# Order of the sums in the recurrence's output batches of a hybrid MLA and RWKV-7 trunk

## The chip, the cores and the metric

The kernel runs on one core of one Trainium2 chip. The metric is the device time of one execution in microseconds, as the median of several runs.

## The reference, cut to what matters

Two layers work on 512 prompt frames and 64 frames of a running stream, with the same weights. A layer is a SwiGLU half-step, a token mixer, cross-attention into 256 memory tokens, and a second SwiGLU half-step. In the mixer eight MLA attention heads stand beside eight RWKV-7 heads. The part at issue is the RWKV-7 recurrence, per head with a 64 by 64 state:

```
def step(S, inp):
    r_t, w_t, k_t, v_t, kk_t, a_t = inp
    sa = einsum('bhvk,bhk->bhv', S, -kk_t)
    S = (S * w_t[:, :, None, :] + sa[..., None] * (kk_t * a_t)[:, :, None, :]
         + v_t[..., None] * k_t[:, :, None, :])
    return S, einsum('bhvk,bhk->bhv', S, r_t)
```

The output y of each token is the state after that token, read with r. The eight heads' outputs are then normalised, gated and projected together with the attention's.

## The kernel before, in words

All activations lie transposed, features on the partitions and the 576 frames along the free dimension. Nearly all large matmuls are done as three products of split operands (high by high, high by low, low by high; `mm3`, lines 314 to 316), and the weights are split as they arrive (lines 246 and 247).

The recurrence of `mixer` is done by chunks of 64 frames. There are nine of them in a layer: first the one of the running stream, which starts from a stored state, and then the eight of the prompt, of which the first has no state. `prepare(c)` makes what doesn't depend on the state: the masked products `A`, an inverse by three rounds (tiles `nd`, `R`, `RF`), the transposed keys `bkt` and the values, brought to the other half of the partitions (`VS`, `UV`). `advance(c, ...)` is the chain from state to state: `pz` (A with VS), copied to `Z`; `pu` (RF with Z), copied to `UV` in two halves, by ScalarE and by VectorE; `pS` (bkt with UV), which with the old state becomes the new one (`S`); and the outputs `py`, copied to `yt`. `py` has two terms where there is an old state: the state read with `ck` (64 rows are summed over), and `UV` read with `A` (128 rows). Then come the mean and the squares of the outputs (`pc`, `p8`).

Each of these products is a `batch`: eight heads, as four pairs `p4` with two heads `e` each. A head has 64 columns of one bank of PSUM, at `p4 * 64`, on the upper or the lower half of the partitions by `e`. So a batch is one bank with eight sums of 64 by 64 numbers. All are plain f32 matmuls; each leaves two records in the trace.

The banks of the chain and of the outputs come from one tag, `sm`, with two buffers; those of `prepare` from `pp` with one. While the chain runs, `more(n)` draws pieces of MLA attention and of the memory's keys and values into the same program order (tags `g`, `sc`, `tp`, `po`). The order of the instructions on each engine is not that of the program text: a planner lays it out at compile time by its own model of the times, with the program's order as priority, and each engine then works through its own queue in that order.

Of the kernel before, what the change touches and what calls it, by code (L numbers as in the profile page):

```python
# [131 lines left out]
def build(tc, I, O):  # L132
    nc = tc.nc
    PE, ACT, DVE, POOL, SP = nc.tensor, nc.scalar, nc.vector, nc.gpsimd, nc.sync
# [23 lines left out]
    def tile_(shape, tag, dt):  # L158
        pool, n = tags[tag]
        return pool.tile(shape, dt, tag=tag, name=tag, bufs=n)  # L160
# [7 lines left out]
    def ps1(tag="sm"):  # L168
        return tile_([128, 512], tag, F32)
# [6 lines left out]
    def half(e):  # L176
        return slice(64 * e, 64 * e + 64)
# [439 lines left out]
    def mixer(l, V, xn):  # L617
# [374 lines left out]

        def batch(tag, *terms):

            p = ps1(tag)
            for p4 in range(4):
                for e in range(2):
                    o = p[half(e), p4 * 64:p4 * 64 + 64]
                    for n, f in enumerate(terms):
                        PE.matmul(o, *f(p4, e), start=(n == 0), stop=(n == len(terms) - 1))  # L1000
            return p[:, 0:256].rearrange("p (h t) -> p h t", h=4)

        def quads(tag):
# [7 lines left out]
        def prepare(c):  # L1011
# [9 lines left out]
            for e in range(2):  # L1021
# [3 lines left out]
                DVE.tensor_tensor(out=A[:, e], in0=p, in1=C("mA").rearrange("p (e n) -> p e n", e=2)[:, e].unsqueeze(1).to_broadcast([128, 4, 128]), op=ALU.mult)  # L1025

            pn = batch("pp", lambda p4, e: (A[half(e), e, p4, aa], DD[half(e), p4]))
            nd = st([128, 4, 64], "nd")
            ACT.activation(out=nd, in_=pn, func=AF.Copy)
            R = DT  # L1030
            for j in range(3):
                p = batch("pp", lambda p4, e: (nd[half(e), p4], R[half(e), p4]))
                R = st([128, 4, 64], "RF" if j == 2 else "R")
                DVE.tensor_tensor(out=R, in0=p, in1=DT, op=ALU.add)
# [25 lines left out]
        def advance(c, ck, bkt, A, R, VS, UV, S, VSn):  # L1060
# [3 lines left out]
            if S is None:  # L1064
                pz = batch("sm", lambda p4, e: (A[half(1 - e), e, p4, aa], VS[half(1 - e), e, p4]))
            else:
                pz = batch("sm", lambda p4, e: (A[:, e, p4, aa], VS[:, e, p4]))
# [72 lines left out]
        for p4 in range(4):  # L1140
            t1 = st([128, T], "t1")
            for s in hs:
                p = ps1()[:, 0:HT]
# [6 lines left out]
            for s, tag in zip(hs, ("pp", "po")):  # L1150
                p = ps1(tag)[:, 0:HT]
# [346 lines left out]
```

## Time and profile before

| | |
|---|---|
| median of 3 runs | 2917.13 us (2910.97 to 2923.18) |
| profiled execution, its own time | 2916.22 us |
| its span | 2914.5 us |
| matmul, share of the span | 96% |
| VectorE, ScalarE, GpSimd | 73%, 47%, 13% |
| mean granted TensorE clock | 0.973 |

The profile is that of one execution. PE is TensorE's matmuls and PEld its weight loads, which overlap with them; DVE is VectorE, ACT is ScalarE, POOL is GpSimd. A busy share says that the engine had an instruction in work, not that it worked at full rate. The granted clock is told as a share of the full 2.4 GHz. Times in the trace are in us from the start of the span.

### The profile page before, as it was taken

To read this page: it belongs to the slowest core of one execution; us is meant where nothing else is said; L and a number is where in the kernel's file an instruction comes from. 1 tells how busy PE (TensorE), PEld (TensorE's weight loads), DVE (VectorE), ACT (ScalarE), POOL (GpSimd) and SP (SyncE) were. 2 spreads that over 40 slices of the span, in tenths; PEclk is the share of its full clock that TensorE was granted. 3 is DMA by queue.
4 is the path that set the end of the run, shared out by engine and by line. 5 is a ranking of instruction groups with operands and counts; after the bars stand their busy time and mean duration, and the time that the engine had idled before them with its cause. 6 is when DMAs were issued, how large, how long until landed. Compare 5 with 4: busy or idle time off the path is not lost.

```text
span 2914.5 us, 56004 instructions
## 1 busy us (share of the span) xinstructions
PE 2808.8 (96%) x22188; PEld 2681.1 (92%) x22188; DVE 2132.0 (73%) x4216; ACT 1370.1 (47%) x2813; POOL 380.6 (13%) x461
## 2 busy tenths in 40 slices
PE   6999999889999999999989999998999999899998
PEld 6999999878889889999989999997888899899998
DVE  8887776865657579777787777668555666787776
ACT  5544455344544545444444444653545445444444
POOL 4000013510000031000130000254000000400000
PEclk8999999989999999999989999998999999999999
DMA  4333333552233222222213222346332332222222
GB/s 168 109 124 105 102 124 110 139 143 81 86 102 123 70 80 87 95 95 88 81 58 102 87 87 91 131 107 159 110 90 88 110 120 66 79 88 87 89 94 69
DMA packets 187576, 293.22 MB, mean 101 GB/s; under 512 B 87066, under 2 KB 113050, under 8 KB 187138
## 3 DMA queue, kind: packets, MB, share of 16 engines
q1 hardware_dynamic: 185010, 285.46, 31.8%
q0 software_dynamic: 2304, 4.20, 0.5%
q8 instruction: 174, 2.85, 0.4%
q14 instruction: 88, 0.72, 0.1%
HBM read 250.36 MB, written 41.63 MB: 100 GB/s over the span
## 4 chain that ended last, share of the span: by engine, by line
PE 71%; DVE 4%; DMA 1%; ACT 1%; issue 1%; POOL 1%; SPq 0%; DVEq 0%; POOLq 0%; ACTq 0%
PE b L316 13%; PE b L314 13%; PE b L315 13%; PE sm L1000 4%; PE g L314 3%; PE g L316 3%; PE g L315 3%; PE mm L314 2%; PE mm L315 2%; PE mm L316 2%; PE pp L1000 2%; PE sc L314 1%; PE pp L1024 1%; PE sc L316 1%; PE sc L315 1%
## 5 line engine op out<-in xcount | busy, mean ns | idle before, releaser
L246 ACT ACTIVATE whi<-wraw 128x512 fp32r<-128x512 f32 (+1 forms) x520 | 321.4, 623 | 486.1 <-PE b L315 226.7
L316 PE MATMUL b<-s,wlo 128*128 128x288 f32 x1536 | 450.2, 295 | 0.0
L315 PE MATMUL b<-s,whi 128*128 128x288 f32 x1536 | 448.8, 293 | 0.0
L314 PE MATMUL b<-s,whi 128*128 128x288 f32 x1536 | 447.9, 295 | 0.0
L247 DVE TENSOR_TENSOR wlo<-wraw,whi 128x512 fp32r<-128x512 f32 (+1 forms) x484 | 342.8, 711 | 116.1 <-ACT whi L246 97.0
L314 PE MATMUL b<-xnh,whi 128*128 128x288 f32 x1152 | 345.6, 309 | 36.4 <-ACT xnh L246 15.1
L315 PE MATMUL b<-xnl,whi 128*128 128x288 f32 x1152 | 350.4, 305 | 11.8 <-DVE xnl L247 7.8
L316 PE MATMUL b<-xnh,wlo 128*128 128x288 f32 x1152 | 346.2, 302 | 0.0
L315 PEld LDWEIGHTS b<-s,whi 128*128 128x128 f32 x1536 | 288.5, 188 | 0.0
L316 PEld LDWEIGHTS b<-s,wlo 128*128 128x128 f32 x1536 | 288.1, 188 | 0.0
L314 PEld LDWEIGHTS b<-s,whi 128*128 128x128 f32 x1536 | 286.6, 188 | 0.0
L314 PEld LDWEIGHTS b<-xnh,whi 128*128 128x128 f32 x1152 | 222.0, 196 | 43.6 <-ACT xnh L246 16.9
L378 POOL TENSOR_TENSOR nacc<-nacc,nsq 128x576 f32<-128x576 f32 x40 | 64.9, 1623 | 1405.1 <-ACT nsq L376 838.4
L594 DVE SCALAR_TENSOR_TENSOR x<-b,x 128x288 f32<-128x288 f32 x320 | 144.4, 454 | 140.2 <-PE b L316 139.8
L315 PEld LDWEIGHTS b<-xnl,whi 128*128 128x128 f32 x1152 | 225.8, 196 | 15.7 <-DVE xnl L247 10.1
L316 PEld LDWEIGHTS b<-xnh,wlo 128*128 128x128 f32 x1152 | 225.5, 196 | 0.1
L315 PE MATMUL b<-s,sh 128*128 128x288 f32 x704 | 208.6, 296 | 0.0
L314 PE MATMUL b<-s,sh 128*128 128x288 f32 x704 | 207.7, 295 | 0.0
L316 PE MATMUL b<-s,sl 128*128 128x288 f32 x704 | 207.7, 295 | 0.0
L314 PE MATMUL mm<-xnh,whi 128*128 128x288 f32 x688 | 205.4, 299 | 1.1 <-ACT xnh L370 1.0
L246 ACT ACTIVATE whi<-S 128x512 fp32r<-128x512 f32 x188 | 118.0, 630 | 182.2 <-PE b L315 180.3
L316 PE MATMUL mm<-xnh,wlo 128*128 128x288 f32 x688 | 203.5, 296 | 0.0
(455 smaller groups left out, 7623.6 us busy)
## 6 DMA issues: line engine op xcount, KB each, us to landing
wraw<-in_wgu SPq DMA_DIRECT2D x136, 512.0 KB
wraw<-in_wds SPq DMA_DIRECT2D x60, 512.0 KB
sraw<-in_wgu SPq DMA_DIRECT2D x40, 512.0 KB
wraw<-in_win SPq DMA_DIRECT2D x36, 512.0 KB
sraw<-in_wds SPq DMA_DIRECT2D x20, 512.0 KB
wraw<-in_wmk SPq DMA_DIRECT2D x16, 512.0 KB
wraw<-in_wmv SPq DMA_DIRECT2D x16, 512.0 KB
wraw<-in_wout SPq DMA_DIRECT2D x32, 256.0 KB
```

Of the source, the lines that this page charges most:

```text
L246: ACT.activation(out=h, in_=src, func=AF.Copy)
L247: by.tensor_tensor(out=lo, in0=src, in1=h.bitcast(F32), op=ALU.subtract)
L314: PE.matmul(out, wh, ah, start=first, stop=False, **kw)
L315: PE.matmul(out, wh, al, start=False, stop=False, **kw)
L316: PE.matmul(out, wl, ah, start=False, stop=last, **kw)
L378: e.tensor_tensor(out=acc, in0=acc, in1=s, op=ALU.add)
L594: DVE.scalar_tensor_tensor(out=o, in0=p, scalar=0.5, in1=o, op0=ALU.mult, op1=ALU.add)
L1000: PE.matmul(o, *f(p4, e), start=(n == 0), stop=(n == len(terms) - 1))
L1024: PE.matmul(p[:, p4], bk[half(e), p4], ck[half(e), p4, 0:128], start=True, stop=True)
```

## The change

`batch` sums over its terms in the outermost loop, not in the innermost: the bank gets the first term of all eight heads, and then the second term of all eight. The mark that opens a sum (`start`) clears what the bank remembers of earlier writes for its half of the partitions; it is now set on the first matmul of each half alone, since the sums of all heads are open at the same time, and the others write without it. For a batch of one term the order of the matmuls stays what it was.

```
         def batch(tag, *terms):
 
+
             p = ps1(tag)
-            for p4 in range(4):
-                for e in range(2):
-                    o = p[half(e), p4 * 64:p4 * 64 + 64]
-                    for n, f in enumerate(terms):
-                        PE.matmul(o, *f(p4, e), start=(n == 0), stop=(n == len(terms) - 1))
+            for n, f in enumerate(terms):
+                for p4 in range(4):
+                    for e in range(2):
+                        o = p[half(e), p4 * 64:p4 * 64 + 64]
+                        PE.matmul(o, *f(p4, e), start=(n == 0 and p4 == 0), stop=(n == len(terms) - 1), skip_group_check=True)
             return p[:, 0:256].rearrange("p (h t) -> p h t", h=4)
```

## Rows read from the trace of the kernel before

**Rows 1.** The page's head: span, and of each engine busy time, share, instructions.

```profile
span 2914.5 us, 56004 instructions
...
PE 2808.8 (96%) x22188; PEld 2681.1 (92%) x22188; DVE 2132.0 (73%) x4216; ACT 1370.1 (47%) x2813; POOL 380.6 (13%) x461
```

**Rows 2.** Windows over the two recurrences: length, busy by engine, clock, DMA.

```profile
630.00:860.00 230.00, 227.31 (x2372) 193.60 (x2371) 129.12 (x339) 116.11 (x313) 17.14 (x40) 0.96 0.29 89
2065.00:2300.00 235.00, 232.30 (x2453) 199.06 (x2453) 135.41 (x357) 122.57 (x327) 17.18 (x40) 0.98 0.30 92
```

**Rows 3.** Waits of TensorE, layer 0's recurrence: sum in us, times, longest.

```profile
PE pp L1045 <- ACT bkt L1039: 0.7, 1, 0.7
```

**Rows 4.** Tile sm, layer 0's recurrence: who waited for it (us, times).

```profile
  ACT yt L1090: 17.7, 7
  ACT UV L1071: 6.9, 6
```

**Rows 5.** The helper's line in the whole trace: durations in ns, min/median/max.

```profile
L1000 PE MATMUL sm<-A,UV x288: 222/222/367, 638.0 to 2292.7; 128*64 128x64 f32 x144
...
L1000 PE MATMUL sm<-ck,S x256: 218/267/366, 637.8 to 2292.4; 64*64 64x64 f32 x128
```

**Rows 6.** TensorE in order of time around one output batch: start, us, line, tiles.

```profile
714.28 0.68 PE L1000 MATMUL pp<-DI,A 64*64 64x64 f32 x16
714.89 0.69 PE L1000 MATMUL sm<-UV,bkt 128*64 128x64 f32 x16
715.50 0.33 PE L1000 MATMUL sm<-ck,S 64*64 64x64 f32 x2
715.76 0.33 PE L1000 MATMUL sm<-A,UV 128*64 128x64 f32 x2
...
719.35 0.33 PE L1000 MATMUL sm<-A,UV 128*64 128x64 f32 x2
719.62 1.22 PE L969 MATMUL po<-ptf,vs 128*128 128x128 f32 x4
```

**Rows 7.** Windows over all two-term batches, 32 pieces: length, matmul busy, clock, DMA.

```profile
637.75:641.50 3.75, 3.75 (x31) 0.94 0.12 39
642.41:643.16 0.75, 0.75 (x8) 0.50 0.00 0
...
851.62:855.06 3.44, 3.44 (x21) 0.65 0.42 122
...
2242.32:2243.53 1.21, 1.21 (x7) 0.50 0.00 0
...
sum 65.64, PE 65.64; mean PE 2.05
```

**Rows 8.** Windows over the five stretches at half clock, columns as in rows 2.

```profile
641.00:647.85 6.85, 6.85 (x52) 5.69 (x52) 2.50 (x7) 1.84 (x5) 0.00 (x0) 0.50 0.19 57
719.55:726.40 6.85, 6.85 (x45) 5.40 (x45) 1.12 (x2) 2.27 (x7) 0.00 (x0) 0.50 0.21 57
852.80:859.65 6.85, 6.85 (x30) 5.97 (x31) 4.13 (x6) 3.27 (x7) 0.00 (x0) 0.51 0.13 41
...
sum 30.75, PE 30.75 PEld 26.49 DVE 12.00 ACT 10.92 POOL 0.00; mean PE 6.15 PEld 5.30 DVE 2.40 ACT 2.18 POOL 0.00
```

**Rows 9.** TensorE in order of time around a lone group of the chain.

```profile
666.66 0.28 PE L314 MATMUL g<-x,whi 128*128 128x256 f32 x1
666.78 0.28 PE L315 MATMUL g<-x,whi 128*128 128x256 f32 x1
666.99 0.33 PE L1000 MATMUL sm<-UV,bkt 128*64 128x64 f32 x2
667.25 0.39 PE L316 MATMUL g<-x,wlo 128*128 128x256 f32 x1
667.47 0.28 PE L314 MATMUL g<-x,whi 128*128 128x256 f32 x1
```

**Rows 10.** TensorE in order of time: four matmuls onto one output.

```profile
861.15 0.61 PE L1098 MATMUL sm<-yq,cst 128*8 128x64 f32 x8
861.69 0.40 PE L315 MATMUL pp<-ginl,wgh 128*128 128x288 f32 x1
```

## The prediction

> **What bounds the kernel now.** I read the page first. TensorE's matmuls fill 2808.8 of 2914.5 us, VectorE 2132.0, ScalarE 1370.1 [rows 1]: the span is TensorE's queue in order, and an edit counts by what it takes out of that queue or puts in, as long as the other engines keep up. The change sits in the recurrence of the mixer, once per layer, so I next read the two stretches of it by windows: matmuls fill 227.31 of 230.00 us in layer 0 and 232.30 of 235.00 in layer 1, VectorE stands at 129 to 135, ScalarE at 116 to 123, the DMA engines at a share of 0.29 to 0.30 [rows 2]. The reader should see that this stretch is called a recurrence, but is not bound by its chain of steps: attention and memory matmuls fill the gaps and TensorE is idle 5.4 us in 465. The view of waits says the same from both sides: the longest single wait of TensorE there is 0.7 us [rows 3], while ScalarE's copy of the output bank waited 17.7 us in seven times for TensorE, and its copy of UV 6.9 us in six [rows 4]. The other engines wait for TensorE.
>
> Then I read what the edited helper issues. Its line has 256 records that multiply S by ck and 288 that multiply UV by A [rows 5]. Each f32 matmul leaves two records, so 16 batches of 8 state terms and 18 batches of 8 UV terms: in 16 of the 18 output batches (8 chunks of 9, in two layers) there are two terms, and the first chunk of the prompt has no state and one term.
>
> Last I read such a batch in order of time; it is the key view. Ahead of it run two one-term batches of 16 records, one of tiles 64 by 64 and one of tiles 128 by 64. From start to start of the next row they take 714.89 - 714.28 = 0.61 us and 715.50 - 714.89 = 0.61 us. Then comes the output batch, in which the two shapes alternate, two records of the one and two of the other. Its rows follow each other at 0.26 us (715.50, 715.76, ...) and 16 of them last from 715.50 to 719.62, 4.12 us [rows 6]. The same 32 records in two uniform batches would be 1.22 us. So the alternation costs 2.9 us, and no wait is printed in it: TensorE counts as busy.
>
> **The change part by part.** Removed: no instruction. Added: none; copies, DMAs and tiles stay. Moved: in the 16 two-term batches the eight state terms come first, and then the eight UV terms. In the one-term batches (seven per chunk, and the output batch of the first prompt chunk) the loop gives the same matmuls in the same order; only the mark that opens a sum stands on the first matmul of each half instead of on all eight. I cost that at nothing. The bound: in the alternating batch the state rows carry the mark and the UV rows don't, and both take 0.26 us [rows 6], so the mark has no price of its own that can be seen.
>
> *The batches.* I cut the stretches of the 16 two-term batches out of TensorE's timeline, without the pieces where other batches cut in. That makes 32 pieces with 65.64 us in sum [rows 7], 4.10 us for each batch. After the change each is one uniform batch of 64 by 64 tiles and one of 128 by 64 tiles, at 0.61 us each [rows 6]: 16 x 1.22 = 19.5 us. Gain: 65.6 - 19.5 = 46.1 us. Most of these batches are cut once by a batch of the next chunk's preparation. A cut in a uniform batch may cost an extra change of shape, (0.26 - 0.05) or about 0.2 us, 0.05 us being about what a group adds within a batch ((0.61 - 0.26) / 7, from [rows 6]). 16 cuts would be 3.4 us; I take 2, with 0 and 3.4 as bounds.
>
> *The clock.* The second thing that I read is the granted clock by stretches. There are five in which it falls to its half level, 1.2 of 2.4 GHz: 6.85 us from 641.00, and four more, with 30.75 us in sum and the matmul row full through all of it [rows 8]. Each begins inside a two-term batch or at its end: 641.00 lies in the piece 637.75 to 641.50 and 852.80 in the piece 851.62 to 855.06 [rows 7], 719.55 at the end of the one of [rows 6]. The mean clocks of the two recurrences, 0.96 and 0.98 [rows 2], leave room for no more (0.04 x 2 x 230 = 18 us against three of 6.85, 0.02 x 2 x 235 = 9.4 against 6.80 and 3.40, at two digits). I read this as one mechanism: the alternating batch streams few columns for 4 us, and the clock falls. The uniform batch is over in 1.2 us, so I expect the five stretches gone. Of the 30.75 us, four pieces of the batches already stand in the sum above: by their clock 0.45 + 0.75 + 2.41 + 1.21 = 4.8 us (twice the missing share of the clock times the length, [rows 7]). The other 26 us of work would take half as long, so 13 us come back. Bounds 0 (the falls only move) and 13.
>
> *What is late next.* TensorE reaches its next instructions 2.9 us earlier after each batch, and some of their inputs are then not ready: the scores go over VectorE and ScalarE before the transposes, and the preparation's bank is copied by ScalarE. Below: nothing, since the other engines are those that wait [rows 4]. Above: one wait as long as the longest there is, 0.7 us [rows 3], for each of the 16 batches, 11 us. I take 0.25 us each, 4 us, nearer to nothing, because VectorE and ScalarE fill 57% and 51% of the two stretches [rows 2], and 65% and 58% if each gets 29 us shorter. No DMA is moved, and the weight loads behind the recurrence run at a share of 0.3, so I cost them at nothing; the FFN after it is TensorE's queue again [rows 1].
>
> Sum against the profiled execution, 2916.2 us (span 2914.5): 2916.2 - 46.1 - 13 + 2 + 4 = 2863 us. It lies 0.9 us below the median of the three runs, 2917.13, so nothing is corrected for that.
>
> *A rule against the change.* The uniform batch alternates between the upper and the lower half of the rows, and both halves write one bank. The row for it is the 64 by 64 batch ahead of the output batch, which does just that and takes 0.61 us for its eight groups [rows 6]. The Trainium skill, page TensorEngine Tiling (Array Packing), section Restrictions and Gotchas, says that different row tiles cannot use the same PSUM bank at the same time; by it the state terms would still run one after another, with no more than a part of the gain. The trace doesn't agree as far as these batches show it.
>
> **The rivals.**
> *The clock doesn't come back.* The preparation and the chain have other small batches, and the five falls may belong to the whole group of them. For it: only 5 of 16 batches have a fall behind them, so the batch alone doesn't decide. Against: none of the stretches begins elsewhere. Time: 2916.2 - 46.1 + 2 + 4 = 2876 us. The Trainium skill, page TensorE: Matmul & The Clock Gate, section HAM oscillation, ties falls to gaps in which the engine is idle; by that rule the batch, which has no gap, isn't the cause. The rows have the matmul row full at the falls [rows 8], so the trace doesn't agree.
>
> *The two halves block each other in the bank.* Then the eight state groups stay at 0.26 us, 2.06 instead of 0.61: the gain shrinks by 16 x 1.45 = 23 us, and 2876 becomes 2899, or 2886 with the clock. Against: the one-term batch of the same shape [rows 6]. This is what the rule named above, of the Trainium skill's page TensorEngine Tiling (Array Packing), would make of it.
>
> *The gain turns into waits.* It is not the change of shape that costs 0.26 us, but the UV term's adding onto columns that the group before has just written. This is taken away too, since eight groups then lie between. What speaks against it as the cause: four matmuls that add onto one and the same output take 861.69 - 861.15 = 0.54 us, 0.14 each [rows 10]. Only if each batch had a new wait of 2.9 us would the time stay at 2916; the waits of TensorE there [rows 3] are a quarter of that at most.
>
> *Slower.* The order of the queue is not the loop's: a planner lays it out. The state terms need only S and ck, and if it scatters them over the attention matmuls, each lone group costs more than now. Such a lone group stands at 666.99: it comes 0.21 us after the row before it, lasts 0.26, and the row behind it takes 0.22 [rows 9]. In a stream whose rows otherwise follow at 0.12 us that is 0.26 + 0.09 + 0.10 = 0.45 us, against 0.26 in the batch of now. All 16 groups scattered would be 7.2 instead of 4.1 us, 16 x 3.1 = 50 us more: 2966. It decides from 9 scattered groups of 16 (9 x 0.45 = 4.05). Against: the output bank comes from a pair, and the batch gets the one that the two UV copies must have read first; so the state terms can't start before UV is there, and state and UV terms are ready together.
>
> **How the numbers follow.** Forecast (2850 to 2871): 0.66. Clock not given back: 0.18. Banks block: 0.04. Waits or scattering that eat about all: 0.04 within 0.5%. Rest of faster cases, between these: 0.05. Slower: 0.03. A measurement of this kernel tells about 0.5%, 14.6 us, from no change (its runs lie within 12 us of each other). So faster 0.93, same 0.04, slower 0.03. The predicted time is 2863. The range: below, all costs at nothing and 13 us from the clock give 2857, less 6 us of scatter of a run and some for a better fill, 2849; above, no clock and 11 us of waits and 3.4 of cuts give 2884.5, so 2886.
>
> **What would show it.** In the trace after: two rows of 16 records for the output batch, 64 by 64 and then 128 by 64, together near 1.2 us (cut once at most); the median of the 256 records that read ck down from 0.267 us [rows 5] to about 0.22; no stretch at half clock in the two recurrences; both recurrences some 26 to 30 us shorter; PE's idle time in them up by a few us. The prediction is wrong if the alternation is still there in the order of the queue, if the uniform rows still come at 0.26 us, or if TensorE's waits grow by tens of us.

## The result and the profile after

The changed kernel takes 2868.68 us (median of 4 runs, 2865.1 to 2871.15) against 2918.59 us (2910.97 to 2923.18): ratio 0.9839, 95% interval 0.9818 to 0.986. The forecast was 2863 us, with 2849 to 2886 as its range. By the medians it is 49.9 us faster. The profiled execution took 2865.1 us, the lowest of its four runs and 51.1 us less than that of before, where 53 were forecast.

The head of the page of the changed kernel, which answers to [rows 1]:

```profile
span 2863.2 us, 56005 instructions
...
PE 2753.5 (96%) x22188; PEld 2641.8 (92%) x22188; DVE 2129.2 (74%) x4216; ACT 1368.5 (48%) x2813; POOL 383.1 (13%) x461
```

The matmul row lost 55 us with the same number of matmuls, 4 us more than the span, and the other engines kept their work. The same output batch as in [rows 6], in order of time on TensorE, in the changed kernel:

```profile
708.04 0.68 PE L1001 MATMUL pp<-DI,A 64*64 64x64 f32 x16
708.65 0.69 PE L1001 MATMUL sm<-UV,bkt 128*64 128x64 f32 x16
709.26 0.68 PE L1001 MATMUL sm<-ck,S 64*64 64x64 f32 x16
709.88 0.69 PE L1001 MATMUL sm<-A,UV 128*64 128x64 f32 x16
710.49 0.71 PE L969 MATMUL po<-ptf,vs 128*128 128x128 f32 x4
```

From 709.26 to 710.49 are 1.23 us; before they were 4.12. The windows over all two-term batches of the changed kernel (35 pieces, since other batches cut in; columns: length, matmul busy, clock, DMA):

```profile
639.80:640.91 1.11, 1.11 (x30) 1.00 0.07 15
...
829.08:830.39 1.31, 0.94 (x20) 1.00 0.29 99
...
sum 23.79, PE 23.04; mean PE 0.66
```

23.8 us stand against the 65.64 of [rows 7], and the clock is 1.00 in each piece. Two of the pieces hold a wait, as the second one shown. The third view is the recurrence as a whole, from the first output batch of a layer to its last, TensorE alone; first the kernel before, then the changed one:

```profile
637.75:855.06 217.31, 214.70 (x2260) 0.96 0.29 89
2079.28:2292.84 213.56, 210.97 (x2261) 0.98 0.30 91
sum 430.87, PE 425.67; mean PE 212.83
```

```profile
639.80:830.39 190.59, 187.50 (x2261) 1.00 0.33 100
2051.65:2242.02 190.37, 187.29 (x2260) 1.00 0.33 100
sum 380.96, PE 374.78; mean PE 187.39
```

So 430.87 - 380.96 = 49.9 us of the 51.3 by which the span got shorter lie here. The clock is back at 1.00 in both, and the time without a matmul went from 5.20 to 6.18 us. What remains, 1.4 us, is the sum of shifts outside: layer 0's first output batch comes 2.05 us later (639.80 against 637.75), the stretch between the recurrences is 1221.26 us against 1224.22, and the end 621.18 against 621.66. Two of the five stretches at half clock reach beyond the windows of before: 852.80 to 859.65, where the window ends at 855.06, and the last one, which comes right behind 2292.84. So a part of the clock's gain lies outside; it is worked out below.

Two of the waits for TensorE are much shorter now. For the helper's line in the whole trace (us, times), first the kernel before, then the changed one:

```profile
  ACT yt L1090: 33.9, 13
  DVE R L1034: 32.6, 20
```

```profile
  ACT Z L1069: 13.5, 16
  ACT UV L1072: 12.8, 12
  DVE R L1035: 9.1, 11
...
  ACT yt L1091: 4.4, 4
```

The chain's copies to Z and UV waited the same 13.5 and 12.8 us in the whole trace of before. ScalarE's copy of the outputs, `yt`, went from 33.9 to 4.4, and VectorE's sums `R` of the preparation, whose batches often cut into an output batch, from 32.6 to 9.1.

### The profile page after: what moved, and what is told of

Its sections match the earlier page's. It is cut to its first block, busy times and chain, and to the rows that moved or that the text cites. A ratio compares the mean times of both kernels' runs of the same rounds, so it can differ in the third digit from the quotient of the medians.

```text
span 2863.2 us, 56005 instructions
## 1 busy us (share of the span) xinstructions
PE 2753.5 (96%) x22188; PEld 2641.8 (92%) x22188; DVE 2129.2 (74%) x4216; ACT 1368.5 (48%) x2813; POOL 383.1 (13%) x461
## 4 chain that ended last, share of the span: by engine, by line
PE 89%; DVE 6%; ACT 1%; issue 1%; DMA 1%; POOL 0%; SPq 0%; DVEq 0%; ACTq 0%; POOLq 0%
PE b L314 18%; PE b L316 18%; PE b L315 18%; PE mm L314 4%; PE mm L315 3%; PE g L314 3%; PE mm L316 3%; PE g L315 3%; PE g L316 3%; PE sm L1001 2%; PE pp L1001 2%; PE sc L314 2%; PE pp L1025 1%; PE sc L316 1%; PE sc L315 1%
## 5 line engine op out<-in xcount | busy, mean ns | idle before, releaser
L315 PEld LDWEIGHTS b<-xnl,whi 128*128 128x128 f32 x1152 | 225.4, 196 | 16.8 <-DVE xnl L247 11.3
```

The source lines that it names most:

```text
L315: PE.matmul(out, wh, al, start=False, stop=False, **kw)
```

## The experiments

Two explanations fit the result equally. By the first, a change of the tile shape on TensorE costs the time. By the second, the UV term waits because it adds onto columns that the group before it has just written. A third candidate is the marks. In all nine kernels the planner was free to lay the queue anew; on VectorE, ScalarE and GpSimd the kernel before and e1, e2, e3, e6, e7 and e9 have the order of the changed kernel. Each ratio is to runs of the kernel before that were measured beside that experiment; their median was 2913.19 us for e1 to e4, 2918.16 for e5 to e8 and 2916.09 for e9, so medians of different groups compare to some 5 us only. The fourth column is the sum over all output batches with their pieces (the two one-term ones, 1.34 us, included), from TensorE's timeline of each profile, by start to start of the next row; it is good to about 0.3 us, since records of neighbouring batches mix at the edges.

| kernel | median us | ratio to before, 95% | output batches us | falls of the clock in the recurrences |
|---|---|---|---|---|
| before | 2918.59 | | 67.05 | 5 |
| changed | 2868.68 | 0.9839 (0.9818 to 0.986) | 25.1 | 0 |
| e1_marks | 2916.02 | 1.001 (0.9995 to 1.0024) | 65.4 | 3, shorter |
| e2_oneshape | 2862.15 | 0.9835 (0.9817 to 0.9853) | 23.4 | 0 |
| e3_pairs | 2880.15 | 0.989 (0.9867 to 0.9913) | 36.7 | 0 |
| e4_lag | 2894.84 | 0.9951 (0.9931 to 0.9972) | 53.4 | 1 |
| e5_thrice | 2917.87 | 0.9995 (0.998 to 1.001) | 68.1 | 0 |
| e6_ufirst | 2868.17 | 0.9824 (0.9798 to 0.985) | 24.1 | 0 |
| e7_fours | 2876.14 | 0.9858 (0.9833 to 0.9882) | 29.9 | 0 |
| e8_hoist | 2869.74 | 0.9833 (0.9805 to 0.9861) | 24.9 | 0 |
| e9_halves | 2876.46 | 0.9861 (0.9833 to 0.9888) | 32.5 | 0 |

**e1_marks: the marks alone.**

```
-            for n, f in enumerate(terms):
-                for p4 in range(4):
-                    for e in range(2):
+            for p4 in range(4):
+                for e in range(2):
+                    for n, f in enumerate(terms):
```

> The changed kernel with the loops put back to head by head, so that only the new opening marks are left of the change. If the marks cost and bring nothing and the order of the shapes is what counts, it runs as the kernel before: 2905 to 2930 us, the 16 output batches about 65 us in sum, some falls of the clock (2 to 7) right behind them. If the marks (15 of 16 fewer openings per batch) brought the gain: about 2869 us.

It ran as the kernel before. The marks (eight in a batch before, two now, not "15 of 16 fewer") are no part of the gain, and the gain is the order's.

**e2_oneshape: head by head, one shape.** From the kernel before:

```
-                ys.insert(0, lambda p4, e: (S[half(e), p4], ck[half(e), p4, rr]))
+                ys.insert(0, lambda p4, e: (UV[:, e, p4], A[:, e, p4, rr]))
```

> The kernel before, head by head, but the state term (64 rows) is replaced by a second copy of the UV term (128 rows), so the state read is left out of the outputs. Each head's two terms still add onto the columns just written, but all tiles of a batch have one shape. If changing the shape costs the time: the batches take about 1.2 to 1.5 us each instead of 4.1 and the time is near that of the changed kernel, 2862 to 2875 us, with no falls of the clock behind them. If adding onto the columns that were just written costs it: about 4 us per batch and 2905 to 2930 us.

It ran as the changed kernel. The same batch in its TensorE timeline:

```profile
710.72 0.69 PE L1000 MATMUL sm<-UV,bkt 128*64 128x64 f32 x16
711.23 1.15 PE L1000 MATMUL sm<-A,UV 128*64 128x64 f32 x32
712.31 0.71 PE L969 MATMUL po<-ptf,vs 128*128 128x128 f32 x4
```

Sixteen groups of 128 by 64, each second one onto the columns of the group before, take 1.08 us in one run. Adding onto fresh columns costs nothing that shows here. The second explanation falls.

**e3_pairs, e7_fours and e4_lag: other numbers of changes.** They differ from the changed kernel only in the order of (term n, group g) in a two-term batch:

```
e3:  [(n, 2 * q + e) for q in range(4) for n in range(2) for e in range(2)]
e7:  [(n, 4 * q + e) for q in range(2) for n in range(2) for e in range(4)]
e4:  [(n, g) for i in range(10) for n, g in ((0, i), (1, i - 2)) if 0 <= g < 8]
```

> The changed kernel with two heads of the state term, two heads of the UV term, and so on: 8 changes of shape in a batch in place of 16 before and 2 after, and never two terms of a head in a row. Change of shape theory: 8 runs at 0.26 + 0.05 us are 2.5 us a batch against 1.5 after and 4.1 before, so 16 us over the changed kernel, 2881 to 2890 us, perhaps a fall of the clock or two. If adding onto the columns just written is the cost: as the changed kernel, 2865 to 2872 us.

> The changed kernel with four heads of the one term and four of the other in turn: 4 runs of one shape in a batch, between after (2) and the pairs (8). Change of shape theory: two runs more at 0.2 us each, 16 x 0.4 = 6 us over the changed kernel, 2871 to 2878 us, no falls of the clock. Otherwise as the changed kernel, 2865 to 2872 us.

> The changed kernel with the shapes alternating again, but the UV term of a head two heads behind its state term: three state groups, then one and one in turn, then three UV groups. 12 runs of one shape, and no group adds onto columns that one of the two groups before it wrote. Change of shape theory: 12 x 0.26 + 4 x 0.05 = 3.3 us a batch, 1.8 over the changed kernel, 29 us over 16 batches and up to 8 from the clock: 2895 to 2910 us. Adding onto the columns just written: 2865 to 2875 us.

All three are slower than the changed kernel, and by what their batches took. Over the changed kernel the batches have 11.6, 4.8 and 28.2 us more, and the two recurrences, cut as above, 12.0, 5.7 and 28.9. The medians are 11.5, 7.5 and 26.2 us higher; by the ratios it is 15, 6 and 33. e4_lag hardly differs from the kernel before in what it does, only that no sum is continued at once, and it keeps the larger part of the loss: again the shape and not the columns. Its time is just below what was expected. e3_pairs came out better than expected, clearly so in its batches (11.6 us for 16). Here is why, in its timeline:

```profile
713.45 0.33 PE L1001 MATMUL sm<-ck,S 64*64 64x64 f32 x4
713.71 0.34 PE L1001 MATMUL sm<-A,UV 128*64 128x64 f32 x4
713.98 0.33 PE L1001 MATMUL sm<-ck,S 64*64 64x64 f32 x4
```

and in that of e7_fours:

```profile
712.02 0.45 PE L1001 MATMUL sm<-ck,S 64*64 64x64 f32 x8
712.39 0.45 PE L1001 MATMUL sm<-A,UV 128*64 128x64 f32 x8
712.78 0.45 PE L1001 MATMUL sm<-ck,S 64*64 64x64 f32 x8
```

and of e4_lag:

```profile
711.10 0.44 PE L1001 MATMUL sm<-ck,S 64*64 64x64 f32 x6
711.47 0.33 PE L1001 MATMUL sm<-A,UV 128*64 128x64 f32 x2
711.73 0.32 PE L1001 MATMUL sm<-ck,S 64*64 64x64 f32 x2
```

A run of one group (two records) takes 0.26 us, and a run of two groups takes 0.26 us too. Three or four take 0.37 to 0.39, and eight 0.61. So the price of a run is about 0.15 us for the change and 0.115 us for every two groups begun: the second of two groups is free. The two prices are an estimate, fitted to these rows; no row shows the change by itself.

**e9_halves: is the free one the neighbour in the other half?** The groups of each term in the order 0, 2, 4, 6 (upper half of the output's partitions) and 1, 3, 5, 7 (lower half), in the two-term batches alone:

```
for n in range(2) for g in (0, 2, 4, 6, 1, 3, 5, 7)
```

> The changed kernel with the eight heads of each term in another order, in the two-term batches alone: the four of the one half of the partitions first, and then the four of the other half. Shapes and their changes stay. Runs so far took 0.26 us for one group or for two and about 0.115 us more for each further two, as if the neighbour in the other half ran beside. If that is so, four groups of one half in a row lose it: up to 0.35 us more for each of 32 runs, 2873 to 2881 us. If a group costs 0.06 us whichever half it is in: as the changed kernel, 2865 to 2872 us.

```profile
709.34 0.69 PE L1001 MATMUL sm<-UV,bkt 128*64 128x64 f32 x16
709.95 0.96 PE L1001 MATMUL sm<-ck,S 64*64 64x64 f32 x16
710.84 0.97 PE L1001 MATMUL sm<-A,UV 128*64 128x64 f32 x16
711.74 0.49 PE L969 MATMUL po<-ptf,vs 128*128 128x128 f32 x2
```

0.89 and 0.90 us for each run instead of 0.61, with the same eight groups and the same changes of shape; the batches in sum 7.4 us longer, the two recurrences 7.7. Groups of the two halves do run beside each other where they are neighbours in the queue.

**e5_thrice: long without alternation.** Each two-term batch three times over:

```
-            for n, f in enumerate(terms):
+            for n, f in [(n, f) for r in range(3 if len(terms) == 2 else 1) for n, f in enumerate(terms)]:
```

> The changed kernel with each two-term output batch done three times over in the same bank, in the uniform order; the third gives the result. TensorE then works on small f32 matmuls for about as long as in the alternating batch of before (3 x 1.22 to 1.5 us against 4.1). If the clock falls because of the alternation: no falls inside or behind the batches, and 32 x 1.22 = 39 us more than the changed kernel, 2903 to 2918 us. If any 4 us of small f32 matmuls make it fall: several falls behind the batches as in the kernel before, and some 8 us more, 2911 to 2926 us.

It took as long as the kernel before, and its batches have as many us, 66.8 for 16 against 65.64. The time lies in both ranges and decides nothing; the clock does. It is 1.00 in both recurrences:

```profile
639.53:852.04 212.51, 211.29 (x2764) 1.00 0.29 90
2079.42:2291.97 212.55, 211.32 (x2764) 1.00 0.29 89
```

The two recurrences are 425.06 us here against 430.87 before; that the whole is no shorter comes from the stretches outside them. The mean clock of its ten runs is 0.977 to 0.981, that of the kernel before beside them 0.969 to 0.977. So the same time spent on small f32 matmuls didn't bring the clock down where the shapes don't alternate. One reserve: most of its batches are cut by attention matmuls. Of 48 batches that alternate group by group or nearly so (before, e1, e4), 9 have a fall inside them or at their end; of the batches in the eight other kernels none has.

**e6_ufirst and e8_hoist: is there more to be had?**

```
e6:  -                ys.insert(0, lambda p4, e: (S[half(e), p4], ck[half(e), p4, rr]))
     +                ys.append(lambda p4, e: (S[half(e), p4], ck[half(e), p4, rr]))
e8:  +            py = ps1("sm")
     +            if S is not None:
     +                term(py, lambda p4, e: (S[half(e), p4], ck[half(e), p4, rr]), True, False)
                  pS = batch("sm", lambda p4, e: (bkt[:, p4, half(e)], UV[:, e, p4]))
     +            term(py, lambda p4, e: (UV[:, e, p4], A[:, e, p4, rr]), S is None, True)
```

> The changed kernel with the two terms in the other order: UV term first, state term second. The batch ahead has the UV term's shape and the batch behind often the state term's, so one or two changes of shape fall away per batch, at 0.1 to 0.2 us. Change of shape theory: 2 to 5 us below the changed kernel, 2862 to 2868 us. If only the number of changes inside the batch counts: the same, 2865 to 2872 us.

> The changed kernel with the state terms of the output batch put ahead of the product of UV with the keys in the program, so that they can run while UV is copied. The bank is opened earlier. If they fill a wait: a few us less, 2860 to 2867 us. As the recurrence has hardly a wait in TensorE's queue, and the planner lays single groups between other shapes, I rather expect no gain or a loss of some us: 2866 to 2880 us.

Neither can be told from the changed kernel by its time. In the trace of e6_ufirst the saved change is there: the UV term follows `pS`, which has its shape, at once, and both batches take 0.51 + 0.57 us up to the state term:

```profile
705.62 0.69 PE L1001 MATMUL sm<-UV,bkt 128*64 128x64 f32 x16
706.13 0.64 PE L1001 MATMUL sm<-A,UV 128*64 128x64 f32 x16
706.70 0.68 PE L1001 MATMUL sm<-ck,S 64*64 64x64 f32 x16
```

That is about 0.15 us for a batch, and the two recurrences of this profile together are 3 us shorter (377.98 against 380.96). The runs spread more than that.

## Why the prediction was right, step by step

*The bound.* TensorE's queue in the recurrence, with next to no waits: right. What left the queue there left the span.

*The batches.* Forecast 65.6 - 19.5 with 2 us for cuts, a gain of 44.1 us; measured 65.64 - 23.04 = 42.6 (matmul time of the pieces; the other 0.75 of their 23.79 us are two waits, counted below). A batch that isn't cut takes 1.23 us as forecast. The error is in the cuts, 23.04 - 19.5 = 3.5 us instead of 2, at the upper bound of 3.4: 35 pieces are 19 cuts, where 16 were counted, and some batches are cut more than once. One batch that is cut, in the changed kernel:

```profile
2220.52 0.44 PE L1001 MATMUL sm<-ck,S 64*64 64x64 f32 x6
2220.89 0.50 PE L314 MATMUL sc<-kfh,qh 128*128 128x512 f32 x1
...
2221.79 0.56 PE L1001 MATMUL sm<-ck,S 64*64 64x64 f32 x10
2222.28 0.56 PE L1001 MATMUL sm<-A,UV 128*64 128x64 f32 x10
2222.77 0.33 PE L1001 MATMUL pp<-DI,A 64*64 64x64 f32 x2
```

6 and 10 records of the state term take 0.37 + 0.49 us, 0.25 more than in one piece.

*What the alternation costs.* The prediction took all of it for the change of shape. There are two parts: by the estimate above, of the 2.9 us for a batch 14 changes at 0.15 are 2.1, and 8 x 0.115 = 0.9 are the neighbour in the other half that is missing when the shape changes after each group. That there are two is shown by e3 and e9; how they share the 2.9 us is the estimate's. That sized e3's expectation too high by some 4 us in its batches, but not the forecast, since the 0.61 us of the uniform batch were read from a row. The Trainium skill, page TensorEngine Tiling (Array Packing), section Tiling Modes, says that changing the tiling mode drains TensorE, and that different tiles can load weights and multiply in parallel; the 0.15 and the 0.26 us for one group or two agree with both, though no row shows a drain as such.

*The clock.* All five falls are gone, as forecast, and e5 and the other runs tie them to the alternation. How an alternating batch comes to have a fall or not (5, 3 and 1 of 16) stays open. The size was a little off: forecast 13 us, measured about 11.3. Inside the windows the clock's gain is what the batches and the waits leave, 49.9 - 42.6 + 1.0 = 8.3 us. But only 22.9 of the 30.75 us at half clock lie in these windows; 7.8 come behind the last output batch of each layer. There TensorE has the same matmuls in the same order in both kernels. Up to the four matmuls onto one output (for layer 0 before, the first of [rows 10]) the rows are, before and then changed:

```profile
2298.44 0.61 PE L1098 MATMUL sm<-yq,cst 128*8 128x64 f32 x8
```

```profile
834.99 0.61 PE L1099 MATMUL sm<-yq,cst 128*8 128x64 f32 x8
2246.65 0.61 PE L1099 MATMUL sm<-yq,cst 128*8 128x64 f32 x8
```

From the end of the windows these are 861.15 - 855.06 = 6.09 us against 834.99 - 830.39 = 4.60 in layer 0, and 2298.44 - 2292.84 = 5.60 against 2246.65 - 2242.02 = 4.63 in layer 1. That is 2.5 us, and 3.0 without a new wait of 0.26 us in each. So 8.3 + 3.0 = 11.3.

The rest of the error is in the step that took all work at half clock for twice as long. The same matmuls, from the 128 by 128 product behind the output batch of [rows 6] (710.49 in the changed kernel) up to the squares' matmuls, before and then changed:

```profile
720.77 1.12 PE L1000 MATMUL pp<-DI,nd 64*64 64x64 f32 x16
721.82 0.42 PE L954 MATMUL tp<-cst,pexp 64*64 64x64 f32 x2
...
726.74 0.61 PE L1098 MATMUL sm<-yq,cst 128*8 128x64 f32 x8
```

```profile
711.13 0.68 PE L1001 MATMUL pp<-DI,nd 64*64 64x64 f32 x16
711.74 0.30 PE L954 MATMUL tp<-cst,pexp 64*64 64x64 f32 x2
...
714.68 0.61 PE L1099 MATMUL sm<-yq,cst 128*8 128x64 f32 x8
```

They take 726.74 - 719.62 = 7.12 us in the kernel before, nearly all at half clock, and 714.68 - 710.49 = 4.19 us in the changed one, a factor of 1.7; the batch that reads nd in them goes from 1.05 to 0.61 us. So a us at half clock gives back about 0.41. The 26 us gave 11.3, 0.43 each, and e1 says the same: its recurrences are 8.1 us shorter than those of before (422.79 against 430.87) with 3.4 us at half clock in the windows instead of 22.9, 0.41 for each. Why it isn't 0.5 stays open.

*What is late next.* Forecast 4 us, measured 1.0 in the two recurrences (5.20 to 6.18 us without a matmul) and 0.5 right behind them. The new waits aren't spread over the 16 batches: behind the last one of each layer TensorE waits 0.37 us for ScalarE's `yah` and 0.26 for VectorE's `yal`. Elsewhere the neighbours waited for TensorE, and the copy `yt` simply waits 29.5 us less.

*The rivals.* The banks don't block: the state term takes 0.61 us, and e9 shows the two halves run beside each other in one bank; the rule of the Trainium skill named in the prediction (page TensorEngine Tiling (Array Packing), section Restrictions and Gotchas) doesn't hold for these batches. That sums wait for fresh columns: fell with e2 and e4. That the state terms are scattered as lone groups: they aren't, a batch is in 1 to 4 pieces. The clock came back.

*The signs.* The prediction looked for batches cut once at most, which some aren't, and for 26 to 30 us less in each recurrence. Layer 0 has 26.7 (217.31 to 190.59), but layer 1 only 23.2 (213.56 to 190.37), since it had less at half clock to give back: 6.8 us in its window against 16.1. The sum of the two was near what the forecast needs; its even split was not.

So the sum was 53.1 us and the span got 51.3 shorter: the batches gave 1.5 less and the clock 1.7 less, the waits took 2.5 less, and the other shifts outside the recurrences, of which no run shows the cause, took 1.1. The closeness of the total is partly luck: the errors cancel.

## What to carry to other kernels

Look at small f32 matmuls by start to start, not by their busy time: here TensorE was called busy through 2.9 us of loss in each batch. Where one bank takes terms of different contraction length, sum term by term, with the two halves of the output alternating inside a term, and open the bank's sums with one mark for each half. A gain in the queue is worth its full length only where the rows around it show that the other engines wait for that queue, as here.

## What the runs showed of the hardware that was not expected

Two groups of 64 columns whose outputs lie in different halves of the partitions cost as much as one: 0.26 us for a run of one or of two, for tiles of 64 by 64 and of 128 by 64. Put in the order of the halves, eight groups take 0.89 us instead of 0.61.

The clock fell with the matmul row full (6.85 of 6.85 us in [rows 8]); in e1 too, three times for 3.4 us, each behind an alternating batch. The Trainium skill, page TensorE: Matmul & The Clock Gate, section HAM oscillation, ties such falls to gaps in which the engine is idle. No such gap is printed in these rows, but they can't decide it: the matmul row also counts the 2.9 us that an alternating batch loses as busy, so TensorE may stand still there unseen. The prediction went too far where it said that the trace doesn't agree.
